# The closing stage of a streaming encoder layer: two groups of inner tiles in one sum, and a norm placed between products

## The chip, the cores and the metric

The kernel runs on one core of one Trainium2 chip. The metric is device time in microseconds (us) of one execution. TensorE (PE) multiplies matrices, VectorE (DVE), ScalarE (ACT) and GpSimd (POOL) work elementwise, and SyncE (SP) issues the transfers (DMAs).

## What is computed

One inference step of one encoder layer for 1088 tokens of width 1024 in float32. After the attention part the second feed-forward block closes the layer:

```python
h = h + 0.5 * rmsnorm(swiglu(rmsnorm(h, g_pre_ff2), w_gate2, w_up2, w_down2), g_post_ff2)
return rmsnorm(h, g_final), rows

def swiglu(x, w_gate, w_up, w_down):
    return (jax.nn.silu(x @ w_gate) * (x @ w_up)) @ w_down
```

The inner width of the block is 2816, so the hidden product has 22 tiles of 128 rows. Two norms follow the down projection: post2, which needs the whole down projection of a token, and the final one, which needs the whole of h.

## The kernel before

Activations lie transposed: features on the 128 partitions (KT = 8 tiles), tokens along the free axis. Tokens are split into G1 (576) and G2 (512). Each operand of a product is split into a high part (ACT cast, L139) and a low part (DVE subtraction, L140), so one product of tiles is three matmuls: high by high, high by low, low by high. All matmuls are issued at L154.

`ffn` is a generator that runs a feed-forward block. For each inner tile `mi` it loads four units of gate and up weights (`unit`: a DMA into one of four `wr` buffers, then cast and subtraction into one of eight `wl`/`wh` buffers), runs 48 matmuls of 512 columns, forms silu(gate) * up with three ACT and two DVE steps (L361 to L365) and splits the result into `hh`/`hl`. Inner tiles come in groups of GROUP = 4. `down` adds a group to the result y: for each of eight feature tiles `dt` it sums the group's tiles in one PSUM bank (`f`, three banks in rotation), and DVE adds the bank to y (L319). A group's `down` comes after the first tile of the next group. The last group has only the tiles 20 and 21; `down_last` adds it, and there the block of G2 is cut into two halves of 256 tokens (`step`), first half first.

The block of G2 is the last one of the kernel (`third` in `body`). When all its products are laid out, `last` lays out the norms: for each half, square and sum of y over the eight tiles (L214 to L218), a matmul with ones to sum over partitions, reciprocal root on ACT (L227, L230), the post2 scaling and the residual in place (L276 on DVE, L277 on DVE or, for odd tiles, POOL), a second norm of the result, the final scaling into an `out` buffer (L1099, two buffers of two tiles each) and its DMA (L1101). In the second half the sums over tiles are made by PE (`rms_pe`, L238 to L241).

Much earlier in the program, at the end of the attention part of G2, `L.scaled` prepares the input of that block: eight scalings (L263) into `e` buffers (three), each followed by a cast and a subtraction, on POOL for odd tiles. Another block's products run beside it as filler.

A scheduler of the language sets the order of each engine's queue from an estimate of when things are ready; the engines then run their queues strictly in that order. In the names that follow, numbers are of buffers: one number of `f` is one bank's sum.

Of the kernel before, what the change touches and what calls it, by code (L numbers as in the profile page):

```python
# [7 lines left out]
F32 = mybir.dt.float32  # L8
F32R = mybir.dt.float32r
AF = mybir.ActivationFunctionType  # L10
ALU = mybir.AluOpType
# [4 lines left out]
P = 128  # L16
D = 1024
KT = D // P
H = KT // 2
# [6 lines left out]
FT = DFF // P  # L26
# [12 lines left out]
G2 = (576, 512, 512)  # L39
# [3 lines left out]
GROUP = 4  # L43
# [22 lines left out]
class Layer:  # L66
# [225 lines left out]
    def unit(self, pool, src):  # L292
        lo = pool.tile([P, 512], F32R, name="wl")
        hi = pool.tile([P, 512], F32R, name="wh")
        raw = pool.tile([P, 512], F32, name="wr")
        self.nc.sync.dma_start(raw, src)
        self.split(hi, lo, x=raw)
        return hi, lo

    def ffn(self, pool, tmp, n, g, xhi, xlo, y, end=None, tail=None):  # L300
        nc, a = self.nc, self.a
        _, T, C = g
        wg, wu, wd = a[f"wg{n}"], a[f"wu{n}"], a[f"wd{n}"]
        pend = []

        def units(src):
            return [self.unit(pool, src[:, i:i + 512]) for i in (0, 512)]

        def product(part, ws, first, dt, c0, C):
            ps = self.bank_f()  # L310
            ks = slice(dt % H * P, dt % H * P + P)
            for i, ((wh, wl), (_, hh, hl)) in enumerate(zip(ws, part)):
                yield from self.steps(ps[:, :C], wh[:, ks], wl[:, ks], hh[:, c0:c0 + C], hl[:, c0:c0 + C],
                                      i == 0, i == len(part) - 1)
            yy = y[:, dt, c0:c0 + C]
            if first:
                nc.scalar.copy(yy, ps[:, :C])
            else:
                nc.vector.tensor_tensor(yy, ps[:, :C], yy, op=ALU.add)  # L319


        def down(part, first):
            for half in range(2):
                ws = [self.unit(pool, wd[mi][:, half * 512:half * 512 + 512]) for mi, _, _ in part]
                for dt in range(half * H, half * H + H):
                    for c0 in range(0, T, C):
                        yield from product(part, ws, first, dt, c0, C)


        def down_last(part, step, beside):  # L330
            ws = [[self.unit(pool, wd[mi][:, half * 512:half * 512 + 512]) for mi, _, _ in part] for half in range(2)]
            if step:
                order = [(dt, c0, step) for c0 in range(0, T, step) for dt in range(KT)]
            else:
                order = [(dt, c0, C) for dt in range(KT) for c0 in range(0, T, C)]
            for dt, c0, n in order:
                for _ in product(part, ws[dt // H], False, dt, c0, n):
                    yield True
                next(beside, None)

        for m in range(0, FT, GROUP):
            part = []
            for mi in range(m, min(m + GROUP, FT)):
                if mi == m + 1 and pend:
                    yield from down(pend.pop(0), m == GROUP)
                gw = units(wg[mi])
                uw = units(wu[mi])
                hh = pool.tile([P, T], F32R, name="hh")
                hl = pool.tile([P, T], F32R, name="hl")
                for c0 in range(0, T, C):  # L350
                    cs = slice(c0, c0 + C)
                    pg = self.bank_f()
                    pu = self.bank_f()
                    for ps, ws in ((pg, gw), (pu, uw)):
                        for k in range(KT):
                            wh, wl = ws[k // H]
                            ks = slice(k % H * P, k % H * P + P)
                            yield from self.steps(ps[:, :C], wh[:, ks], wl[:, ks], xhi[:, k, cs], xlo[:, k, cs],
                                                  k == 0, k == KT - 1)
                    s = tmp()[:, :C]  # L360
                    nc.scalar.activation(s, pg[:, :C], AF.Exp, scale=-1.0)  # L361
                    nc.scalar.activation(s, s, AF.Ln, bias=self.one)
                    nc.scalar.activation(s, s, AF.Exp, scale=-1.0)  # L363
                    nc.vector.tensor_tensor(s, pg[:, :C], s, op=ALU.mult)  # L364
                    nc.vector.tensor_tensor(s, pu[:, :C], s, op=ALU.mult)  # L365
                    self.split(hh[:, cs], hl[:, cs], x=s)
                part.append((mi, hh, hl))
            pend.append(part)
        while end and not self.mixed:
            yield BLOCKED  # L370
        end = end() if end else iter(())
        yield from down_last(pend.pop(0), tail, end)
        self.run(end)


# [638 lines left out]
def body(tc, a, ctx):  # L1014
    nc = tc.nc
    L = Layer(tc, ctx, a)
# [5 lines left out]
    fp = ctx.enter_context(tc.tile_pool(name="ffn", bufs=1))  # L1022
# [6 lines left out]
    F = Stream()  # L1029
# [7 lines left out]
    def pair(pool, T, name):  # L1037
        return pool.tile([P, KT, T], F32R, name=name + "h"), pool.tile([P, KT, T], F32R, name=name + "l")
# [8 lines left out]
    def ytile(T):  # L1047
        return fp.tile([P, KT, T], F32, name="y")
# [21 lines left out]
            nc.sync.dma_start(a["yT"][k * P:k * P + P, t0:t0 + T], o)  # L1070
            t = L.done(t + SLACK * (T / 960 + 0.15))

    def last(gi, y, res, pool, step):

        t0, T, C = groups[gi]
        yT = a["yT"].rearrange("(k p) t -> p k t", p=P)
        for c0 in range(0, T, step):
            cs = slice(c0, c0 + step)
            tmp = lambda: pool.tile([P, step], F32, name="t", bufs=4)

            def norm():

                r = pool.tile([P, step], F32, name="r", bufs=4)
                if c0 + step == T:
                    L.rms_pe(tmp, L.bank_f, [y[:, k, cs] for k in range(KT)], step, r)
                else:
                    for k in range(KT):
                        L.square(tmp, r, y[:, k, cs], k == 0)
                    L.rsqrt(L.bank_f, r, step, D, r)
                return r  # L1090

            r = norm()
            for k in range(KT):
                L.residual(res[:, k, cs], y[:, k, cs], "post2", k, r, None, nc.gpsimd if k % 2 else nc.vector)
            r = norm()
            for k in range(0, KT, 2):
                o = pool.tile([P, 2, step], F32, name="out", bufs=2)
                for i in range(2):
                    nc.vector.scalar_tensor_tensor(o[:, i], y[:, k + i, cs], L.gain("final", k + i), r,  # L1099
                                                   op0=ALU.mult, op1=ALU.mult)  # L1100
                nc.sync.dma_start(yT[:, k:k + 2, t0 + c0:t0 + c0 + step], o)  # L1101

    def premix(tmp, bank, y, T, hi, lo, at):
        r = L.rms(tmp, bank, [y[:, k, :] for k in range(KT)], T, D, at=at)
# [2 lines left out]
    def work(pool, T, n=4):  # L1107

        L.there = L.clock + 6.0

        class W:
            def tile(self, shape, dt, name):
                return pool.tile(shape, dt, name=name, bufs=2)
        return lambda: pool.tile([P, T], F32, name="e", bufs=n), W(), lambda: pool.tile([P, T], F32, name="acc")


    T1, T2 = G1[1], G2[1]
    x1 = pair(fp, T2, "x")
    with tc.tile_pool(name="x0", bufs=1) as xp:
        x0 = pair(xp, T1, "x")  # L1120
        y = ytile(T1)
        half = T1 // 2
        y0 = ytile(T1)
        zero = L.ffn(F, fact, 1, G1, *x0, y0)
        for c0 in (0, half):
            cs = slice(c0, c0 + half)
# [4 lines left out]
            tmp = lambda: xp.tile([P, half], F32, name="t", bufs=5)  # L1131
            r = xp.tile([P, half], F32, name="r", bufs=2)
# [10 lines left out]
        tmp = lambda: xp.tile([P, T2], F32, name="p", bufs=4)  # L1143
        get = streamed(tmp, xT[1])
        r = L.rms(tmp, L.bank_f, (get(k) for k in range(KT)), T2, D)
# [19 lines left out]
    with tc.tile_pool(name="m0", bufs=1) as mp:  # L1165
        tmp, wp, acc = work(mp, T1)
# [7 lines left out]
    tmp, wp, acc = work(mp, T1, 3)  # L1174
    o = pair(mp, T1, "o")
# [11 lines left out]
    with tc.tile_pool(name="m1", bufs=1) as mp:  # L1187
        tmp, wp, acc = work(mp, T2)
# [6 lines left out]
    h = hp.tile([P, KT, T2], F32, name="h")  # L1195
    with tc.tile_pool(name="m2", bufs=1) as mp:
        tmp, wp, acc = work(mp, T2)
        o = pair(mp, T2, "o")
        L.mix_out(wp, tmp, acc, L.bank_m, 1, G2, *o, h, rz)
    lp = ctx.enter_context(tc.tile_pool(name="last", bufs=1))  # L1200
    x3 = pair(lp, T2, "x")
    tmp = lambda: lp.tile([P, T2], F32, name="e", bufs=3)
    L.scaled(tmp, lambda k: h[:, k], "pre2", rz, *x3)
    L.run(second)

    y3 = lp.tile([P, KT, T2], F32, name="y")
    third = L.ffn(F, fact, 2, G2, *x3, y3, tail=T2 // 2)
    L.filler = third
    finish(0, y2, 2, L.bank_m)
    L.run(third)  # L1210
    last(1, y3, h, lp, T2 // 2)


OUTS = {"yT": (D, NTOK), "o_lat": (P, NTOK), "o_kr": (32, NTOK), "o_k": (512, NTOK), "o_v": (NTOK, 512)}
# [87 lines left out]
```

## Time and profile before

| | us |
|---|---|
| three timed runs: lowest, median, highest | 2359.6, 2362.08, 2370.45 |
| the profiled execution's own time | 2356.51 |
| its span, first to last instruction | 2354.7 |
| PE busy in the span | 2265.2 (96%) |
| granted TensorE clock, mean over the span | 0.990 |

The profile is one execution. Busy time of PE is of overlapping matmuls, so a stretch can be filled without a matmul starting at every moment; the distance from one start to the next is the pace. A releaser behind an arrow is what ended a wait.

### The profile page before, as it was taken

The page shows a single profiled execution, that of the slowest core. Times are in us where ns is not written, and L with a number is a line of the kernel's source. Part 1 is how long each engine was busy: PE and PEld are TensorE (multiplying, and loading weights), DVE is VectorE, ACT ScalarE, POOL GpSimd, SP SyncE. Part 2 cuts the span into 40 slices and gives each one's busy share as a digit, 9 for nine tenths or more (in the row PEclk, how much of TensorE's full clock was granted, in tenths as well). Part 3 has the DMA queues.
Part 4 walks back from the last instruction along what each step waited for, and adds up shares of the span by engine and source line. Part 5 has one row for each costly group of instructions (what it writes and reads, how often), then busy time and mean ns, then how long its engine had stood idle before and what let it go on. Part 6 is the DMA issues. An engine that isn't in the chain of part 4 may idle for free.

```text
span 2354.7 us, 37574 instructions
## 1 busy us (share of the span) xinstructions
PE 2265.2 (96%) x13841; PEld 2036.4 (86%) x13841; DVE 1433.7 (61%) x2482; ACT 1283.9 (55%) x2494; POOL 95.8 (4%) x270
## 2 busy tenths in 40 slices
PE   8999999989999999999989999999999989999996
PEld 7999999979987777788878998989898888888884
DVE  5444444764248777846874478878776568344445
ACT  6543333452357777754542588777876445433333
POOL 1000000010000000000110000000000010000001
PEclk9999999999999999999999999999999999999998
DMA  6322222444454434344445532322212334332221
GB/s 208 106 90 90 81 81 84 155 156 143 146 157 123 131 111 126 92 147 131 134 144 176 171 104 82 93 86 86 90 63 97 106 99 147 114 98 99 95 85 36
DMA packets 186615, 268.80 MB, mean 114 GB/s; under 512 B 59216, under 2 KB 68048, under 8 KB 186400
## 3 DMA queue, kind: packets, MB, share of 16 engines
q1 hardware_dynamic: 186432, 266.41, 35.1%
q8 instruction: 109, 1.79, 0.3%
q14 instruction: 74, 0.61, 0.1%
HBM read 227.61 MB, written 40.88 MB: 114 GB/s over the span
## 4 chain that ended last, share of the span: by engine, by line
PE 71%; DVE 11%; ACT 9%; DMA 4%; issue 3%; SPq 1%; POOL 1%; DVEq 0%; ACTq 0%; POOLq 0%
PE f L154 48%; PE s L154 9%; PE v L154 6%; PE t L154 6%; DVE a L613 2%; PE t L158 2%; ACT wh L139 1%; DVE wl L140 1%; ACT a L607 1%; ACT a L609 1%; DVE a L610 1%; ACT a L608 1%; DVE e L263 1%; DVE pl L680 1%; DVE y L276 1%
## 5 line engine op out<-in xcount | busy, mean ns | idle before, releaser
L154 PE MATMUL f<-xh,wh 128*128 128x288 f32 (+1 forms) x2112 | 694.3, 329 | 5.6 <-ACT xh L139 2.8
L154 PE MATMUL f<-xl,wh 128*128 128x288 f32 (+1 forms) x2112 | 695.5, 329 | 2.2 <-POOL xl L140 1.5
L154 PE MATMUL f<-xh,wl 128*128 128x288 f32 (+1 forms) x2112 | 694.7, 329 | 0.0
L139 ACT CAST wh<-wr 128x512 fp32r<-128x512 f32 x638 | 385.1, 619 | 518.1 <-PE f L154 354.7
L140 DVE TENSOR_TENSOR wl<-wr,wh 128x512 fp32r<-128x512 f32 x638 | 435.6, 698 | 256.2 <-ACT wh L139 223.7
L154 PEld LDWEIGHTS f<-xh,wh 128*128 128x128 f32 x2112 | 397.3, 188 | 36.4 <-DVE act L364 3.5
L154 PEld LDWEIGHTS f<-xl,wh 128*128 128x128 f32 x2112 | 397.1, 188 | 33.8 <-POOL xl L140 3.1
L154 PEld LDWEIGHTS f<-xh,wl 128*128 128x128 f32 x2112 | 397.2, 188 | 28.5 <-issue 1.7
L154 PE MATMUL f<-hh,wh 128*128 128x288 f32 (+2 forms) x1072 | 351.0, 328 | 8.4 <-DVE y L319 8.2
L154 PE MATMUL f<-hh,wl 128*128 128x288 f32 (+2 forms) x1072 | 351.0, 328 | 0.0
L154 PE MATMUL f<-hl,wh 128*128 128x288 f32 (+2 forms) x1072 | 350.4, 327 | 0.1
L154 PEld LDWEIGHTS f<-hh,wh 128*128 128x128 f32 x1072 | 201.9, 189 | 24.1 <-DVE y L319 9.8
L154 PEld LDWEIGHTS f<-hl,wh 128*128 128x128 f32 x1072 | 202.2, 189 | 14.5 <-issue 1.0
L154 PEld LDWEIGHTS f<-hh,wl 128*128 128x128 f32 x1072 | 202.1, 189 | 13.6 <-issue 1.0
L319 DVE TENSOR_TENSOR y<-f,y 128x288 f32<-128x288 f32 (+2 forms) x248 | 127.0, 519 | 116.9 <-PE f L154 116.6
L364 DVE TENSOR_TENSOR act<-f,act 128x288 f32<-128x288 f32 (+1 forms) x132 | 70.2, 532 | 121.1 <-ACT act L363 121.0
L680 DVE TENSOR_TENSOR pl<-t,ph 128x384 fp32r<-128x384 f32 (+1 forms) x160 | 98.7, 632 | 28.6 <-ACT ph L679 27.4
L365 DVE TENSOR_TENSOR act<-f,act 128x288 f32<-128x288 f32 (+1 forms) x132 | 70.1, 531 | 65.0 <-PE f L154 61.4
L139 ACT CAST hh<-act 128x288 fp32r<-128x288 f32 (+1 forms) x132 | 65.1, 494 | 78.7 <-DVE act L365 78.4
L154 PE MATMUL v<-pl,v 128*128 128x256 f32 x320 | 89.6, 302 | 14.8 <-DVE pl L680 13.9
L679 ACT CAST ph<-t 128x384 fp32r<-128x384 f32 (+1 forms) x160 | 84.4, 543 | 33.2 <-PE t L158 31.7
L158 PE MATMUL t<-c_ident,a 128*128 128x128 f32 x616 | 91.3, 273 | 4.9 <-ACT a L624 4.8
(316 smaller groups left out, 3476.5 us busy)
## 6 DMA issues: line engine op xcount, KB each, us to landing
wr<-in_wg SPq DMA_DIRECT2D x176, 256.0 KB, 2.7
wr<-in_wu SPq DMA_DIRECT2D x176, 256.0 KB, 3.1
wr<-in_wd SPq DMA_DIRECT2D x176, 256.0 KB, 2.7
wr<-in_win SPq DMA_DIRECT2D x44, 256.0 KB, 3.2
kl<-ks SPq DMA_DIRECT2D x64, 128.0 KB, 2.8
wr<-in_wout SPq DMA_DIRECT2D x32, 256.0 KB, 2.8
h<-y SPq DMA_DIRECT2D x16, 288.0 KB, 2.4
p<-in_xT SPq DMA_DIRECT2D x16, 256.0 KB, 3.2
```

The lines of the kernel that those rows point to most:

```text
L139: nc.scalar.copy(hi, x)
L140: eng.tensor_tensor(lo, x, f(hi), op=ALU.subtract)
L154: self.nc.tensor.matmul(out, lhsT=lhsT, rhs=rhs, start=start, stop=stop)
L158: self.nc.tensor.transpose(out, x, ident)
L263: self.nc.vector.scalar_tensor_tensor(x, src(k), self.gain(name, k), r, op0=ALU.mult, op1=ALU.mult)
L276: nc.vector.scalar_tensor_tensor(y, y, self.gain(name, k), r, op0=ALU.mult, op1=ALU.mult)
L319: nc.vector.tensor_tensor(yy, ps[:, :C], yy, op=ALU.add)
L364: nc.vector.tensor_tensor(s, pg[:, :C], s, op=ALU.mult)
L365: nc.vector.tensor_tensor(s, pu[:, :C], s, op=ALU.mult)
L613: nc.vector.tensor_tensor_scan(a[:, 0:n - 1][:, ::-1], zs[:, 1:n][:, ::-1], a[:, 0:n - 1][:, ::-1], BIG, op0=ALU.add, op1=ALU.subtract)
L679: nc.scalar.copy(ph[:, end:], tr[:, end:])
L680: nc.vector.tensor_tensor(pl[:, end:], tr[:, end:], f(ph[:, end:]), op=ALU.subtract)
```

## The change

1. In the last block (`tail` set), `down` of the group 16 to 19 is not run after tile 20. The groups 16 to 19 and 20 to 21 go to `down_last` together: each bank sums six tiles, 18 matmuls of 256 columns, for 16 banks (eight feature tiles, two halves of the tokens).
2. The twelve weight units that this takes are laid out there. Nine go into the buffer of the input pair of an earlier block (`spare`, free by then; its tiles are called `xh`/`xl`), three into the rotating `wl`/`wh`. The inner result of tile 21 gets a buffer in another pool.
3. `last` becomes a generator and is stepped once after each bank of `down_last`. While the first half's banks run, it lays out the squares of y of that half; between the banks of the second half, the root r1, the post2 step, the squares and the root r2 of the first half, and the squares of the second half. After the last bank: the root r3 of the second half (two matmuls), the final scaling of the first half, then the post2 step, norm and final scaling of the second half.
4. The `out` tiles are taken from the `e` buffers, of which there are now five; so `L.scaled` has five as well.

```diff
+        def unit(src):
+            if not room:
+                return self.unit(pool, src)
+            hi, lo = room.pop(0)
+            raw = pool.tile([P, 512], F32, name="wr")
+            nc.sync.dma_start(raw, src)
+            self.split(hi, lo, x=raw)
+            return hi, lo
...
-                if mi == m + 1 and pend:
+                if mi == m + 1 and pend and not (tail and m + GROUP >= FT):
                     yield from down(pend.pop(0), m == GROUP)
...
-                hh = pool.tile([P, T], F32R, name="hh")
-                hl = pool.tile([P, T], F32R, name="hl")
+                own = inner if inner and mi == FT - 1 else pool
+                hh = own.tile([P, T], F32R, name="hh")
+                hl = own.tile([P, T], F32R, name="hl")
...
-        yield from down_last(pend.pop(0), tail, end)
+        if spare:
+            room.extend(spare())
+        yield from down_last(sum(pend, []), tail, end)
...
+        for k in range(KT):
+            L.square(tmp, r1, y[:, k, one], k == 0)
+            yield
+        ps = None
+        for k in range(KT):
+
+            if k < KT - 1:
+                L.square(tmp, r3, y[:, k, two], k == 0)
+
+            if k == 0:
+                L.rsqrt(L.bank_f, r1, step, D, r1)
+            elif k < 5:
+                for i in range(2 * k - 2, 2 * k):
+                    moved(i, one, r1)
+                    L.square(tmp, r2, y[:, i, one], i == 0)
+            elif k == 6:
+                L.rsqrt(L.bank_f, r2, step, D, r2)
+            if k < KT - 1:
+                yield
+        sq = tmp()
+        nc.scalar.activation(sq, y[:, KT - 1, two], AF.Square)
+        ps = L.bank_f()[:, :step]
+        L.mul(ps, lhsT=L.ones, rhs=r3, start=True, stop=False)
+        L.mul(ps, lhsT=L.ones, rhs=sq, start=False, stop=True)
+        scale(ps, r3)
+        for k in range(0, KT, 2):
+            out(k, one, r2)
+        for k in range(KT):
+            moved(k, two, r3)
+        L.rms_pe(tmp, L.bank_f, [y[:, k, two] for k in range(KT)], step, r4)
+        for k in range(0, KT, 2):
+            out(k, two, r4)
...
-    tmp = lambda: lp.tile([P, T2], F32, name="e", bufs=3)
+    tmp = lambda: lp.tile([P, T2], F32, name="e", bufs=5)
```

`moved` is the post2 step (L276, L277) and `out` the final scaling with its DMA; both are as before.

PE's queue before, where the last group's banks begin (the first of the eight banks of the first half; `hh_24113` is tile 20, `hh_24357` tile 21):

```order
L154 MATMUL f_24441<-hh_24113,wh_24418 128x256
L154 MATMUL f_24441<-hl_24114,wh_24418 128x256
L154 MATMUL f_24441<-hh_24113,wl_24417 128x256
L154 MATMUL f_24449<-hh_24113,wh_24418 128x256
L154 MATMUL f_24449<-hl_24114,wh_24418 128x256
L154 MATMUL f_24449<-hh_24113,wl_24417 128x256
...
L154 MATMUL f_24441<-hh_24357,wh_24424 128x256
L154 MATMUL f_24449<-hh_24357,wh_24424 128x256
```

And after the change, from tile 20 of the first bank on (`hh_24113` is tile 20, `hh_24197` tile 21; twelve matmuls of the tiles 16 to 19 stand ahead of them in that bank):

```order
L154 MATMUL f_24313<-hh_24113,xh_24257 128x256
L154 MATMUL f_24313<-hl_24114,xh_24257 128x256
L154 MATMUL f_24313<-hh_24113,xl_24258 128x256
L154 MATMUL f_24313<-hh_24197,xh_24257 128x256
L154 MATMUL f_24338<-hh_23617,xh_24257 128x256
L154 MATMUL f_24338<-hl_23618,xh_24257 128x256
L154 MATMUL f_24338<-hh_23617,xl_24258 128x256
L154 MATMUL f_24313<-hl_24198,xh_24257 128x256
```

Before, nine matmuls of tile 20 stood ahead of the first one that needs tile 21; now fifteen do, and three more stand between the high and the low part of tile 21.

DVE's queue before, around the last bank of the second half (L319) and the first half's post2 step behind it:

```order
L319 TENSOR_TENSOR y<-f,y 128x256 x6
L276 SCALAR_TENSOR_TENSOR y<-y,c_gains,r 128x256 x2
L277 TENSOR_TENSOR y<-y,h 128x256
L276 SCALAR_TENSOR_TENSOR y<-y,c_gains,r 128x256 x2
L277 TENSOR_TENSOR y<-y,h 128x256
```

After the change, in the second half of the tokens, from the add of its second bank to that of its fifth (L331 is the bank's add, r_24334 the sum for r2, r_24335 that for r3):

```order
L331 TENSOR_TENSOR y_21650<-f_24524,y_21650 128x256
L276 SCALAR_TENSOR_TENSOR y_21650<-y_21650,c_gains_111,r_24333 128x256 x2
L218 TENSOR_TENSOR r_24335<-r_24335,t_24544 128x256
L218 TENSOR_TENSOR r_24334<-r_24334,t_24552 128x256
L277 TENSOR_TENSOR y_21650<-y_21650,h_20311 128x256
L331 TENSOR_TENSOR y_21650<-f_24555,y_21650 128x256
L276 SCALAR_TENSOR_TENSOR y_21650<-y_21650,c_gains_111,r_24333 128x256 x2
...
L331 TENSOR_TENSOR y_21650<-f_24588,y_21650 128x256
```

The post2 step of the first half now stands between the second half's bank adds, where before it stood behind all of them.

DVE's queue at the scaling of the input (L263), before the change and then after it; L319 and L331 are both the filler's bank adds:

```order
L263 SCALAR_TENSOR_TENSOR e<-h,c_gains,rx 128x512 x3
L140 TENSOR_TENSOR xl<-e,xh 128x512
L319 TENSOR_TENSOR y<-f,y 128x288
L263 SCALAR_TENSOR_TENSOR e<-h,c_gains,rx 128x512
...
L319 TENSOR_TENSOR y<-f,y 128x288 x3
L140 TENSOR_TENSOR wl<-wr,wh 128x512 x3
L319 TENSOR_TENSOR y<-f,y 128x288 x4
```

```order
L263 SCALAR_TENSOR_TENSOR e<-h,c_gains,rx 128x512 x3
L140 TENSOR_TENSOR xl<-e,xh 128x512
L263 SCALAR_TENSOR_TENSOR e<-h,c_gains,rx 128x512
...
L331 TENSOR_TENSOR y<-f,y 128x288 x3
L140 TENSOR_TENSOR wl<-wr,wh 128x512 x3
L331 TENSOR_TENSOR y<-f,y 128x288 x5
```

The one bank add that stood among the scalings now stands behind all of them.

## Rows read from the trace of the kernel before

**Rows 1.** The page: the chain that ended last, by engine.

```profile
PE 71%; DVE 11%; ACT 9%; DMA 4%; issue 3%; SPq 1%; POOL 1%; DVEq 0%; ACTq 0%; POOLq 0%
```

**Rows 2.** Stretches: us, busy PE, PEld, DVE, ACT, POOL, granted clock, DMA share, GB/s.

```profile
2272.65:2294.41 21.76, 21.76 (x98) 18.02 (x96) 10.77 (x17) 5.61 (x10) 0.00 (x0) 1.00 0.22 70
2294.41:2305.29 10.88, 10.88 (x50) 9.01 (x48) 2.58 (x4) 2.55 (x4) 0.00 (x0) 1.00 0.00 0
2305.29:2318.08 12.79, 12.53 (x97) 11.72 (x96) 9.59 (x24) 3.79 (x9) 0.00 (x0) 1.00 0.01 1
2318.08:2337.89 19.81, 7.73 (x22) 5.66 (x20) 13.18 (x28) 9.15 (x22) 3.35 (x4) 0.66 0.12 40
2337.89:2354.70 16.81, 5.71 (x16) 3.65 (x16) 9.36 (x20) 4.22 (x10) 3.37 (x4) 0.74 0.23 78
```

**Rows 3.** Timeline of PE: start, us, what; pace of matmuls, and the sums over partitions.

```profile
2309.09 0.28 PE L154 MATMUL f<-hh,wh 128*128 128x256 f32 x1
2309.21 0.28 PE L154 MATMUL f<-hl,wh 128*128 128x256 f32 x1
...
2318.08 0.59 PE L154 MATMUL f<-r,ones 128*128 128x256 f32 x2
```

**Rows 4.** The chain that ended last, in order of time: start, us, what.

```profile
2306.86 0.70 DVE hl L140
...
2318.71 0.48 ACT r L227
...
2319.22 0.42 ACT r L230
...
2329.76 7.15 PE f L154 x18
...
2346.68 0.91 DVE out L1099 x3
```

**Rows 5.** Timeline of DVE, closing stage: start, us, what, count [idle before <-releaser].

```profile
2308.15 1.09 DVE L319 TENSOR_TENSOR y<-f,y 128x256 f32<-128x256 f32 x3 [0.59 <-PE f L154]
...
2319.67 0.88 DVE L276 SCALAR_TENSOR_TENSOR y<-y,c_gains,r 128x256 f32<-128x256 f32 x2 [0.96 <-ACT r L230]
2320.47 0.42 DVE L277 TENSOR_TENSOR y<-y,h 128x256 f32<-128x256 f32 x1
2320.80 1.34 DVE L276 SCALAR_TENSOR_TENSOR y<-y,c_gains,r 128x256 f32<-128x256 f32 x2
...
2325.59 4.12 DVE L218 TENSOR_TENSOR r<-r,t 128x256 f32<-128x256 f32 x7
...
2349.87 1.67 DVE L1099 SCALAR_TENSOR_TENSOR out<-y,c_gains,r 128x256 f32<-128x256 f32 x4 [1.51 <-DMA out_yT<-out]
```

**Rows 6.** Timeline of ACT, and the page's DMA issues: a square, four weight casts, a landing.

```profile
2310.19 0.42 ACT L217 ACTIVATE t<-y 128x256 f32<-128x256 f32 x1 [0.50 <-DVE y L319]
...
2292.34 2.67 ACT L139 CAST wh<-wr 128x512 fp32r<-128x512 f32 x4 [8.22 <-PE f L154]
...
wr<-in_wd SPq DMA_DIRECT2D x176, 256.0 KB, 2.7
```

**Rows 7.** Timeline at the input's scaling, POOL, DVE and PE.

```profile
1906.54 1.29 POOL L140 TENSOR_TENSOR xl<-e,xh 128x512 fp32r<-128x512 f32 x1 [12.26 <-DMA wr<-in_wd]
...
1906.51 0.45 DVE L319 TENSOR_TENSOR y<-f,y 128x288 f32<-128x288 f32 x1
1906.88 1.50 DVE L263 SCALAR_TENSOR_TENSOR e<-h,c_gains,rx 128x512 f32<-128x512 f32 x1
...
1913.74 0.75 DVE L263 SCALAR_TENSOR_TENSOR e<-h,c_gains,rx 128x512 f32<-128x512 f32 x1 [1.16 <-POOL xl L140]
...
1915.01 1.18 DVE L319 TENSOR_TENSOR y<-f,y 128x288 f32<-128x288 f32 x3
...
1915.51 0.61 PE L154 MATMUL f<-hh,wh 128*128 128x288 f32 x1 [6.64 <-DVE y L319]
...
1915.00:1920.00 5.00, 4.49 (x20) 4.49 (x21) 3.70 (x8) 0.14 (x1) 1.28 (x1) 0.56 0.32 101
```

More of the change, by code (lines that the diff above doesn't have):

```diff
@@ L298, in unit, with ffn @@
         return hi, lo
-    def ffn(self, pool, tmp, n, g, xhi, xlo, y, end=None, tail=None):
+    def ffn(self, pool, tmp, n, g, xhi, xlo, y, end=None, tail=None, spare=None, inner=None):
         nc, a = self.nc, self.a
         _, T, C = g
+        room = []
         wg, wu, wd = a[f"wg{n}"], a[f"wu{n}"], a[f"wd{n}"]
         pend = []
+        def unit(src):
[6 more added lines that the diff above has]
+            return hi, lo
         def units(src):
@@ L330, in down_last @@
         def down_last(part, step, beside):
[L331 to L337, printed above, removed]
+            ws = [[unit(wd[mi][:, half * 512:half * 512 + 512]) for mi, _, _ in part] for half in range(2)]
+            order = [(dt, c0) for c0 in range(0, T, step) for dt in range(KT)] if step else \
+                [(dt, c0) for dt in range(KT) for c0 in range(0, T, C)]
+            for dt, c0 in order:
+                for _ in product(part, ws[dt // H], False, dt, c0, step or C):
                     yield True
@@ L1071, in finish, with last @@
             t = L.done(t + SLACK * (T / 960 + 0.15))
-    def last(gi, y, res, pool, step):
+    def last(gi, y, res, pool):
         t0, T, C = groups[gi]
+        step = T // 2
         yT = a["yT"].rearrange("(k p) t -> p k t", p=P)
[L1077 to L1101, printed above, removed]
@@ new lines, in last, with scale, moved, out @@
+        tmp = lambda: pool.tile([P, step], F32, name="t", bufs=4)
+        row = lambda: pool.tile([P, step], F32, name="r", bufs=4)
+        def scale(ps, r):
+            nc.scalar.activation(r, ps, AF.Ln, bias=L.eps, scale=1.0 / D)
+            nc.scalar.activation(r, r, AF.Exp, scale=-0.5)
+        def moved(k, cs, r):
+            L.residual(res[:, k, cs], y[:, k, cs], "post2", k, r, None, nc.gpsimd if k % 2 else nc.vector)
+        def out(k, cs, r):
+            o = pool.tile([P, 2, step], F32, name="e", bufs=5)
+            for i in range(2):
+                nc.vector.scalar_tensor_tensor(o[:, i], y[:, k + i, cs], L.gain("final", k + i), r,
+                                               op0=ALU.mult, op1=ALU.mult)
+            nc.sync.dma_start(yT[:, k:k + 2, t0 + cs.start:t0 + cs.stop], o)
@@ new lines, in last @@
+        one, two = slice(0, step), slice(step, T)
+        r1, r2, r3, r4 = row(), row(), row(), row()
+        for k in range(KT):
[15 more added lines that the diff above has]
+                yield
@@ L1103, in premix @@
+        yield
     def premix(tmp, bank, y, T, hi, lo, at):
@@ L1206, in body, with spare @@
     y3 = lp.tile([P, KT, T2], F32, name="y")
-    third = L.ffn(F, fact, 2, G2, *x3, y3, tail=T2 // 2)
+    def spare():
+        both = [z.rearrange("p k t -> p (k t)") for z in pair(fp, T1, "x")]
+        return [[z[:, i:i + 512] for z in both] for i in range(0, KT * T1, 512)]
+    third = L.ffn(F, fact, 2, G2, *x3, y3, end=lambda: last(1, y3, h, lp), tail=T2 // 2, spare=spare, inner=lp)
     L.filler = third
@@ L1210, in body @@
     L.run(third)
-    last(1, y3, h, lp, T2 // 2)
 OUTS = {"yT": (D, NTOK), "o_lat": (P, NTOK), "o_kr": (32, NTOK), "o_k": (512, NTOK), "o_v": (NTOK, 512)}
```

## The prediction

> **What bounds the kernel now.** The chain by engine comes first [rows 1]: PE makes 71% of it. The change touches the end of the program, so the stretches there come next [rows 2]. Up to 2318.08 PE is full at clock 1.00; from there to the end, 36.6 us, it is not the bound. Two stretches make up that end: 19.81 us until the post2 step of the second half of the tokens begins, and 16.81 us from there. The first one is the whole norm work of the first half and the second half's r3, and in it DVE is busy for 13.18 us. The second half's last products are done at 2318.08, yet its post2 step starts only at 2337.89, because the first half's work stands ahead of it in DVE's queue. The chain in order of time says the same [rows 4]: ACT's root at 2318.71, DVE until the ones-matmul at 2329.76, then PE, then DVE again. While the products of the first half run, DVE and ACT have room: in the 12.79 us of the last group's banks ACT is busy for 3.79. That is the time the change wants to use.
>
> **1. PE's products.** Before: 96 matmuls of 512 columns for the tiles 16 to 19, 21.76 us, and 96 of 256 columns for 20 and 21 in 12.79 us [rows 2]. The pace of 256 columns is 0.12 us [rows 3], so those 96 need 11.5 us; the other 1.3 us is PE waiting for tile 21's split, whose low part ends at 2307.56 [rows 4], 2.27 us after that tile's own products end. After: 288 of 256 columns, 34.56 us, and two ones-matmuls among them (r1, r2) at 0.59 each with their latency [rows 3], together 35.7. Before it was 34.55: plus 1.2 us. The wait for tile 21 should go: the order puts fifteen matmuls ahead of its high part (1.8 us) and nineteen ahead of its low part (2.28 us against 2.27 needed). If that fails, it costs 0.2. The Trainium skill (page TensorE: Matmul & The Clock Gate, section Back-to-back issue gap) gives columns divided by 2.4 GHz plus 2.5 ns for a warm matmul, 109 ns for 256 columns; the row shows 120 and decides; by the page this term would be 2.0 us less.
>
> **2. The weights.** Twelve units (DMA, cast, subtraction) in one go, where before eight were spread over `down` and four followed. Their number and bytes are the same. Nine go into a buffer nobody uses any more, so their casts wait only for a transfer (2.7 us to landing [rows 6]) and not for PE, as the casts of before do (8.22 us [rows 6]). In ACT's order they stand beside tiles 19 and 20, so at least 10.88 us, one tile's time [rows 2], ahead of the first use. Cost 0, covered by tile 21's products; without that cover see the rivals.
>
> **3. The first half's norm beside the second half's products.** Eight banks of 18 matmuls, 2.16 us each. r1's ones-matmul comes after the first of them, r2's after the seventh: 0.59 + 6 x 2.16 = 13.55 us from one to the other. If r2's sum isn't ready by then, PE stands. From r1's ones-matmul: 0.59, root 0.48 + 0.42 [rows 4], 1.5 with handovers. Then DVE: before, the eight scalings and four adds of that step, three of four pairs slowed by a POOL add running beside them (1.34 for a pair against 0.88 [rows 5]), took from 2319.67 to 2325.6, 6.0 us. Between them now stand seven sums for r2, four for r3 and four bank adds, fifteen at about 0.335 (three adds fill 1.09 [rows 5]; the distance of starts): 5.0. The last squares and their chained sums add about 1.0: 4.12 us for seven chained sums [rows 5] makes 0.53 each, and a square takes 0.42 [rows 6]. Sum 13.5 against 13.55. So the wait is between 0 and, with every handover adverse, 1.5 us; I take 0.4, near the lower end, since both sums come out alike. Before that, the bank ring has slack: each of the three banks is needed again two banks (4.3 us) after its end, and DVE's lag never reaches 3.
>
> The four POOL adds of that step run in a stretch where POOL was idle; what they cost is inside the 1.34 rows.
>
> **4. From the last product to the second half's post2 step.** Before 19.81 us [rows 2]. After: three final scalings of the first half stand ahead of the last bank add in DVE's queue. r2's root comes 0.59 + 0.48 + 0.42 and a square between (0.3) after the seventh bank, 1.85 us with handovers; three scalings at 0.4 make 3.05, where the last bank's matmuls end 2.75 after the same point. So the bank add starts 0.3 late; then add 0.42, square 0.42, ones-matmul 0.59, roots 0.90, six handovers of about 0.04: 2.9 us in all. The five final scalings left (2.0 us) fit behind it. With the chance that one of them is late I take 3.3; bounds 2.6 and 5. Gain 19.81 - 3.3 = 16.5 us.
>
> **5. The end.** From 2337.89 to the first final scaling at 2346.68 [rows 4] nothing changes. The eight scalings then took until 2351.5, 4.9 us, with a wait of 1.51 for an `out` buffer on its way to memory [rows 5]. With five `e` buffers they run through: 7 x 0.4 + 0.48 = 3.3. Gain 1.6; if the four transfers of 256 KB, now closer together, queue behind each other, up to 0.7 of it is lost. DMA's 3.1 us at the very end stays.
>
> **6. The five `e` buffers at the input's scaling.** This is a place the change moves without naming it. There PE stood 6.64 us waiting for a filler bank add that is queued behind the scalings [rows 7]. With more buffers the last scaling no longer waits 1.16 us for POOL, so the group of adds may come about 1.0 sooner, near 1914.0. But the single add that stood among the scalings at 1906.51 moves behind them too. It freed a bank, with which PE ran twelve matmuls until 1908.9 (where its wait of 6.64 begins). They now come after the wait: 1.6 us at their pace, nearly 3 at the half clock that follows the wait (0.56 over 1915 to 1920 [rows 7]). Net between 0.5 us won (the clock recovers sooner as PE resumes sooner) and 2 lost; I take 1.0 lost.
>
> **Sum.** +1.2 + 0.4 - 16.5 - 1.6 + 1.0 = -15.5 us. The profiled execution (2356.51; 1.8 around the span of 2354.7) would take 2341.0. It lies 5.6 us under the median of the three runs, which I take as base: 2362.08 - 15.5 = **2346.6 us**, 0.66% faster. About 0.5%, 11.8 us, is what a measurement can tell from no change.
>
> **Rivals.**
> *DVE becomes the bound of the second half.* If POOL slows every DVE operation beside it as it does the scaling of 0.75 us that took 1.50 [rows 7], and not one per POOL add, the 8 + 4 + 15 operations of step 3 grow: four POOL adds of 0.84 us, each holding two operations for about 0.45 more, plus the chain behind them, 4 to 5 us; PE stands at r2's ones-matmul. Gain 11: 2351, within 0.5%. For: 13.5 against 13.55 leaves nothing. Against: only one operation per pair is longer in the rows of before [rows 5].
>
> *The weights come late.* If the casts could not run ahead, six units stand between tile 21 and the first bank: 2.7 for the transfer and 6 x 0.67 of cast (2.67 for four [rows 6]) make 6.7 us of idle PE. Gain 8.8: 2353. Against: the order, and free buffers.
>
> *The clock falls in the long sums, and the kernel gets slower.* The banks of `down_last` wait for DVE in a ring of three, and DVE now does norms between. If the short waits make the clock fall to 1.2 GHz, a matmul of 256 columns takes about 0.21 instead of 0.12 (at clock 0.56 twelve products took nearly twice their time, above). All 288: plus 26 us, 2362.1 + 10.7 = 2373. It is slower than before once more than some 170 of the 288 run so. Against: in the 12.79 us of before, same columns, same ring and a wait of 1.3, the clock was 1.00 [rows 2]; it fell only in long waits. The Trainium skill (the same page, section A second HAM failure mode: psum-queue depth-cycling) says that cycling through banks with short idle pauses can make the clock swing. By that rule this rival would be likely; the trace disagrees.
>
> *The change doesn't do what it says*: the norm still runs after the products, because of a wait that I have not seen. Then 1.2 lost and 1.6 + 1.3 won: 2361, no difference.
>
> **How the numbers follow.** Forecast (gain 13 to 18) 79%; DVE bound 8%; weights late 5%; norm not beside 3%; clock 3%; 2% for what I don't see, half of it slower. Half of the DVE case lies above 11.8 us. Faster 0.82, same 0.14, slower 0.04. The bounds of the terms make the gain 11 to 18; with a base between 2359.6 and 2364 the time is 2341 to 2353; I widen it by 1 on both sides: 2340 to 2354, which leaves out the norm and clock cases and a part of the weights.
>
> **What would show it.** In the changed kernel's trace: matmuls of 256 columns without a break for about 35.5 us; L276 of the first half between bank adds; PE's wait at the second ones-matmul (0 to 1.5, step 3); 3 to 4 us from the last product to the second half's first L276 (step 4); no wait of the final scalings for a DMA (step 5); PE's wait near 1907 to 1915, its length and the clock behind it (step 6). Wrong it would be if PE shows waits of several us among the 288 matmuls, or a clock below 1.00 there, or the end after the last product is longer than 22 us.

## The result, and the profile after

The changed kernel takes 2345.86 us (median of 5 runs, 2343.77 to 2350.41) against 2362.08 before: ratio 0.9935, 95% interval 0.9922 to 0.9949. In a second series the same kernel took 2344.72 us against 2358.91: ratio 0.9945 (0.9931 to 0.9960). The profiled execution took 2345.05 us, its span is 2343.3 against 2354.7.

The two profiled executions can't be compared by their ends alone. At 1894 us, in code that is the same in both, the one of after is already some 5 us later than that of before (before's profiled time lies 5.6 us under its median, after's 0.8), so the changed stretches are compared from a point of their own. For the end of the program this is the start of `down_last`. From there to the end the kernel of after needs 54.41 us (2288.86 to 2343.27). Before, the same products and all that stands behind them took 21.76 us for tiles 16 to 19 and 49.4 from 2305.29 to 2354.70 [rows 2], 71.2 in all. **The gain there is 16.8 us**, and that length hardly varies between executions (54.39 in a second one of the same kernel, 54.41 in one of experiment 6, which has the same end).

Stretches of the kernel after, columns as in [rows 2]: the first half's products, the second half's, from the last product to the second half's post2 step, and the rest.

```profile
2288.86:2306.60 17.74, 17.74 (x148) 17.64 (x147) 7.03 (x16) 3.54 (x8) 0.00 (x0) 1.00 0.00 1
2306.60:2324.60 18.00, 18.00 (x148) 17.89 (x147) 14.16 (x35) 7.34 (x20) 4.42 (x4) 1.00 0.00 1
2324.60:2328.02 3.42, 1.15 (x4) 0.35 (x3) 3.20 (x10) 1.31 (x3) 0.00 (x0) 1.00 0.47 158
2328.02:2343.30 15.28, 5.86 (x16) 3.52 (x16) 9.26 (x20) 4.22 (x10) 3.36 (x4) 0.70 0.31 102
```

PE is busy without a break for both halves of the sum, at clock 1.00, and DVE is busy for 14.16 us inside the second one, with norm work and bank adds (0.42 us each). The stretch of 19.81 us of before [rows 2], counted like it from the ones-matmul behind the last product (2324.42), has shrunk to 3.60.

PE's timeline of after at the two sums of the first half and of r3 (start, us, what). Neither ones-matmul shows a wait:

```profile
2308.44 0.59 PE L154 MATMUL f<-r,ones 128*128 128x256 f32 x2
...
2321.70 0.28 PE L154 MATMUL f<-hh,wl 128*128 128x256 f32 x1
2321.82 0.62 PE L154 MATMUL f<-r,ones 128*128 128x256 f32 x2
...
2324.42 0.63 PE L154 MATMUL f<-r,ones 128*128 128x256 f32 x2
```

DVE's timeline of after (the idle time ahead of an operation and what ended it in brackets): the first half's post2 step between bank adds, r2's last two sums, the final scalings ahead of the last bank add, the second half's first scaling, and the end.

```profile
2310.19 0.88 DVE L276 SCALAR_TENSOR_TENSOR y<-y,c_gains,r 128x256 f32<-128x256 f32 x2 [1.12 <-ACT r L230]
2310.98 0.42 DVE L277 TENSOR_TENSOR y<-y,h 128x256 f32<-128x256 f32 x1
2311.32 0.42 DVE L331 TENSOR_TENSOR y<-f,y 128x256 f32<-128x256 f32 x1
2311.65 1.03 DVE L276 SCALAR_TENSOR_TENSOR y<-y,c_gains,r 128x256 f32<-128x256 f32 x2
...
2320.74 0.95 DVE L218 TENSOR_TENSOR r<-r,t 128x256 f32<-128x256 f32 x2 [0.21 <-ACT t L217]
...
2324.22 1.27 DVE L1105 SCALAR_TENSOR_TENSOR e<-y,c_gains,r 128x256 f32<-128x256 f32 x3
2325.40 0.42 DVE L331 TENSOR_TENSOR y<-f,y 128x256 f32<-128x256 f32 x1
...
2328.02 0.88 DVE L276 SCALAR_TENSOR_TENSOR y<-y,c_gains,r 128x256 f32<-128x256 f32 x2 [0.22 <-ACT r L1097]
...
2336.80 3.26 DVE L1105 SCALAR_TENSOR_TENSOR e<-y,c_gains,r 128x256 f32<-128x256 f32 x8 [2.78 <-ACT r L241]
```

r2's last sum ends at 2321.69, and PE comes to r2's ones-matmul at 2321.82: 0.13 us to spare. The eight final scalings at the end run through in 3.26 us, with no wait for a transfer as in [rows 5].

ACT's timeline of after, around r2's root:

```profile
2322.48 0.48 ACT L227 ACTIVATE r<-f,eps 128x256 f32<-128x256 f32 x1
2323.42 0.42 ACT L217 ACTIVATE t<-y 128x256 f32<-128x256 f32 x1 [0.46 <-DVE y L331]
2323.75 0.40 ACT L230 ACTIVATE r<-r 128x256 f32<-128x256 f32 x1
```

A square of the second half stands between the root's two operations, and it waits 0.46 us for DVE's bank add. That time is on the way to the final scalings at 2324.22 twice over: the root ends at 2324.15, and the sum of that square, which waits for it too, stands right ahead of the scalings in DVE's queue.

```profile
2323.87 0.43 DVE L218 TENSOR_TENSOR r<-r,t 128x256 f32<-128x256 f32 x1 [0.54 <-ACT t L217]
```

The place that the change moves without naming it, the input's scaling: DVE and PE of after, to be read against [rows 7].

```profile
1909.22 2.07 DVE L263 SCALAR_TENSOR_TENSOR e<-h,c_gains,rx 128x512 f32<-128x512 f32 x3
...
1913.07 4.09 DVE L263 SCALAR_TENSOR_TENSOR e<-h,c_gains,rx 128x512 f32<-128x512 f32 x3
...
1917.69 1.75 DVE L263 SCALAR_TENSOR_TENSOR e<-h,c_gains,rx 128x512 f32<-128x512 f32 x1
...
1919.96 1.18 DVE L331 TENSOR_TENSOR y<-f,y 128x288 f32<-128x288 f32 x3
```

```profile
1920.46 0.61 PE L154 MATMUL f<-hh,wh 128*128 128x288 f32 x1 [8.08 <-DVE y L331]
```

Five `e` buffers let three scalings run in one go beside POOL's subtractions (4.09 us for three), and all bank adds come behind the last of them. PE waits 8.08 us instead of 6.64.

### The profile page after: what moved, and what is told of

It is laid out like the page before. It is cut to its first block, busy times and chain, and to the rows that moved or that the text cites. A ratio compares the mean times of both kernels' runs of the same rounds, so it can differ in the third digit from the quotient of the medians.

```text
span 2343.3 us, 37720 instructions
## 1 busy us (share of the span) xinstructions
PE 2260.2 (96%) x13925; PEld 2036.9 (87%) x13925; DVE 1432.1 (61%) x2480; ACT 1282.0 (55%) x2494; POOL 97.1 (4%) x270
## 5 line engine op out<-in xcount | busy, mean ns | idle before, releaser
L139 ACT CAST wh<-wr 128x512 fp32r<-128x512 f32 x629 | 379.9, 619 | 496.3 <-PE f L154 329.6
L154 PE MATMUL f<-hh,wh 128*128 128x288 f32 (+2 forms) x1032 | 337.0, 327 | 9.4 <-DVE y L331 9.3
L154 PE MATMUL f<-hh,wl 128*128 128x288 f32 (+2 forms) x1032 | 337.5, 327 | 0.0
L154 PE MATMUL f<-hl,wh 128*128 128x288 f32 (+2 forms) x1032 | 336.3, 326 | 0.0
L154 PEld LDWEIGHTS f<-hh,wh 128*128 128x128 f32 x1032 | 194.9, 189 | 23.5 <-DVE y L331 10.9
L154 PEld LDWEIGHTS f<-hl,wh 128*128 128x128 f32 x1032 | 195.1, 189 | 13.1 <-issue 1.0
L154 PEld LDWEIGHTS f<-hh,wl 128*128 128x128 f32 x1032 | 195.2, 189 | 12.6 <-issue 1.0
L331 DVE TENSOR_TENSOR y<-f,y 128x288 f32<-128x288 f32 (+2 forms) x240 | 121.6, 513 | 115.9 <-PE f L154 115.4
```

Source lines behind the costliest of these rows:

```text
L139: nc.scalar.copy(hi, x)
L154: self.nc.tensor.matmul(out, lhsT=lhsT, rhs=rhs, start=start, stop=stop)
```

## The experiments

All are edits of the changed kernel. Their stretch from the first product of `down_last` to the end is given beside the total, since it hardly varies between executions of the same end; before and after have 71.2 and 54.4.

**1. The common sum alone.** `down_last` takes the six tiles, but the norm of the first half stands behind all products.

```diff
-    third = L.ffn(F, fact, 2, G2, *x3, y3, end=lambda: last(1, y3, h, lp), tail=T2 // 2, spare=spare, inner=lp)
+    third = L.ffn(F, fact, 2, G2, *x3, y3, tail=T2 // 2, spare=spare, inner=lp)
     L.filler = third
     finish(0, y2, 2, L.bank_m)
     L.run(third)
+    last(1, y3, h, lp, T2 // 2)
```

(`last` is here the one of before, with five `e` buffers for its output.)

> The six tiles are summed together and first half first, as in the changed kernel, but the norm of the first half stands behind all products again, as before. Theory (the gain is the norm work that lies beside products): the 288 products take 34.6 us as before, the stretch from the last product to the second half's post2 step is back at 19 to 20 us, the end keeps its 1.5 us (five out buffers): 1 to 2 us under the kernel before, about 2360.5, no difference that counts. Rival (the common sum itself saves waits and bank adds): 8 us or more under before, 2354 or less.

Measured: 2358.52 us against 2359.55 before in that series, ratio 0.9995 (0.9985 to 1.0004). The chain that ended last, in order of time:

```profile
2254.80 64.85 PE f L154 x421
...
2319.67 0.48 ACT r L227
...
2338.65 0.88 DVE y L276 x2
```

From r1's root to the second half's post2 step it takes 18.98 us, before 19.18 (2318.71 [rows 4] to 2337.89 [rows 2]). The closing stretch is 69.6 us: 1.6 gained, at the end of the output. The common sum by itself brings next to nothing beyond what the five buffers bring; the rival falls.

**2. The norm alone.** Tiles 16 to 19 are summed in `down` again, and only tiles 20 and 21 lie beside the norm.

```diff
-                if mi == m + 1 and pend and not (tail and m + GROUP >= FT):
+                if mi == m + 1 and pend:
...
-    third = L.ffn(F, fact, 2, G2, *x3, y3, end=lambda: last(1, y3, h, lp), tail=T2 // 2, spare=spare, inner=lp)
+    third = L.ffn(F, fact, 2, G2, *x3, y3, end=lambda: last(1, y3, h, lp), tail=T2 // 2)
```

> Tiles 16 to 19 are summed by themselves again, and only tiles 20 and 21 (0.72 us a bank) stand beside the norm of the first half. Theory: r1's to r2's ones-matmul needs 13.5 us of DVE and ACT, and 0.59 + 6 x 0.72 = 4.9 us of products lie between, so PE waits some 8.6 us before the last bank; tile 21's wait of 1.3 is back too. From the end of tile 21: 1.3 + 5.8 + 0.7 + 13.5 + 1.3 + 3.3 = 25.9 us against 32.6 before, and 1.5 at the end: 8 us under before, about 2354, half the gain. Rival (the norm hides as well beside 96 products, the longer sum is not needed): 15 us or more, 2347 or less.

Measured: 2355.78 us against 2359.55, ratio 0.9978 (0.9969 to 0.9988), 2.8 to 7.3 us. PE's timeline:

```profile
2315.42 0.70 PE L154 MATMUL f<-r,ones 128*128 128x256 f32 x2 [0.85 <-DVE r L218]
...
2319.68 0.39 PE L154 MATMUL f<-hh,wh 128*128 128x256 f32 x1 [0.70 <-DVE y L331]
...
2321.81 0.39 PE L154 MATMUL f<-hh,wh 128*128 128x256 f32 x1 [1.15 <-DVE y L331]
...
2329.00 1.22 PE L154 MATMUL f<-r,ones 128*128 128x256 f32 x2 [6.21 <-DVE r L218]
```

From r1's ones-matmul to r2's it takes 13.58 us, where 13.5 was expected, and PE waits in three places (0.70, 1.15, 6.21: 8.06 of the expected 8.6). With tiles 16 to 19 added as before (21.76) the closing stretch is 65.5 us: 5.7 gained, a third and not the half. The 2.6 us that the expectation lacked from tile 21 to the second half's post2 step (28.5 for 25.9) lie almost all at its two ends: r1's ones-matmul already waits 0.85, and the stretch from r2's ones-matmul to the post2 step takes 6.15 instead of 4.6, in which PE, behind the wait of 6.21, runs at half clock.

```profile
2315.42:2329.00 13.58, 5.52 (x39) 4.86 (x39) 12.14 (x30) 6.08 (x17) 3.03 (x4) 0.90 0.00 0
2329.00:2335.15 6.15, 4.58 (x12) 2.95 (x12) 4.29 (x11) 2.32 (x6) 0.00 (x0) 0.50 0.28 95
```

These stretches of the same execution (columns as above) show DVE busy for 12.14 of the 13.58 us, and a clock of 0.50 behind the wait. So the norm needs the long sum as a cover, and the long sum needs the norm: 1.6 and 5.7 apart, 16.8 together, each with the 1.5 us in it that the five buffers give at the end.

**3. r2 one bank earlier.** It measures how much room r2's sum has.

```diff
-            elif k == 6:
+            elif k == 5:
                 L.rsqrt(L.bank_f, r2, step, D, r2)
```

> r2's ones-matmuls stand one bank (2.16 us) earlier in PE's order, all else as in the changed kernel. Theory (r2's sum is ready 0.13 us before PE comes to it, so the fifteen operations of DVE just fit): PE now waits 2.0 us there; the last bank's add no longer stands behind three scalings, which gives back 0.3 to 0.7: 1.3 to 2 us slower than the changed kernel, about 2347.5. Rival (the sum is ready much earlier and DVE only takes its time): a wait under 0.7, and the time is that of the changed kernel or 0.5 us less.

Measured: 2346.95 us, ratio 0.9939 (0.9927 to 0.9952); the closing stretch is 55.9 us, 1.5 more than after. PE:

```profile
2323.12 0.70 PE L154 MATMUL f<-r,ones 128*128 128x256 f32 x2 [1.92 <-DVE r L218]
...
2327.97 0.59 PE L154 MATMUL f<-r,ones 128*128 128x256 f32 x2
```

The wait is 1.92 us; one bank less the 0.13 of room is 2.03. From the last product (r3's ones-matmul, 2327.97) to the second half's post2 step (2330.88) it is 2.9 us instead of 3.6, since r2's scalings no longer stand in front of the last bank add. The fit of step 3 was a close one; the totals of two kernels that differ by 1.5 us could not have shown it.

**4. No POOL in the last norm.** All adds of the last post2 steps on DVE.

```diff
-            L.residual(res[:, k, cs], y[:, k, cs], "post2", k, r, None, nc.gpsimd if k % 2 else nc.vector)
+            L.residual(res[:, k, cs], y[:, k, cs], "post2", k, r, None, nc.vector)
```

> The adds of the last post2 steps all run on DVE, none on POOL, in both halves; all else as in the changed kernel. Theory (a POOL add slows one DVE operation of a pair from 0.48 to 0.94, which is what the adds cost DVE anyway): scalings 0.48 throughout, four adds of 0.335 more on DVE in each half: PE's wait at r2 stays 0, the time from the second half's first scaling to its first final scaling changes by less than 0.7, the total lies within 1 us of the changed kernel, 2345 to 2347. Rival (POOL's share sets the end: without it DVE is the bound): r2 late by 1.3 and the end longer by 1.3, 2348 to 2349.

Measured: 2343.31 us, ratio 0.9926 (0.9913 to 0.9938). In the timeline of DVE the pairs of scalings now take 0.88 us and each pair of adds 0.75; with POOL a pair of scalings took up to 1.34 us and the one add left on DVE 0.41.

```profile
2322.27 0.88 DVE L276 SCALAR_TENSOR_TENSOR y<-y,c_gains,r 128x256 f32<-128x256 f32 x2 [0.22 <-ACT r L1097]
2323.06 0.75 DVE L277 TENSOR_TENSOR y<-y,h 128x256 f32<-128x256 f32 x2
```

The closing stretch is 54.55 us, 0.14 more than after: what POOL takes off DVE it costs DVE in longer scalings. The median lies 2.55 us under after's first one and below the 2345 to 2347 expected, but the stretch that the edit touches doesn't show it, and the intervals overlap; I count it as no difference. PE's timeline shows a wait of 0.19 us at r2, so the room there is used up either way:

```profile
2316.57 0.70 PE L154 MATMUL f<-r,ones 128*128 128x256 f32 x2 [0.19 <-DVE r L218]
```

**5. Three `e` buffers again.** It undoes step 6 and leaves the rest.

```diff
-            o = pool.tile([P, 2, step], F32, name="e", bufs=5)
+            o = pool.tile([P, 2, step], F32, name="out", bufs=3)
...
-    tmp = lambda: lp.tile([P, T2], F32, name="e", bufs=5)
+    tmp = lambda: lp.tile([P, T2], F32, name="e", bufs=3)
```

> Three e buffers at the input's scaling again, and the out tiles of the last norm in three buffers of their own; all else as in the changed kernel. At the scaling one bank add comes back among the scalings. Theory (step 6 costs about 1 us): PE's wait there falls from 8.1 to 6.6 and the stretch up to the first product behind the scalings gets about 1.3 shorter; the end is longer by 0.7, since the fourth pair of the final scalings waits for a transfer: in sum 0 to 1 us faster than the changed kernel, 2345 to 2346. Rival (step 6 costs nothing): 0.7 to 1 slower, 2346.5. The total can hardly tell them apart, the two places in the trace can.

Beside it ran the changed kernel once more:

> The changed kernel itself, beside the other runs of this series: 2344 to 2348 us, ratio 0.9935 as before.

Measured: 2344.21 us against 2344.72 for the changed kernel (and 2358.91 before), ratios 0.9937 (0.9926 to 0.9949) and 0.9945 (0.9931 to 0.9960): no difference. PE's wait at the scaling is 6.64 us again, and the next product there comes 1.4 us sooner, measured against the changed kernel on the same chip (3.8 us ahead of it in front of the scaling, 5.2 behind). But at 2007 us the lead is down to 3.4: it was given back. Where it went is told below. At the end the last pair of scalings waits for an output buffer:

```profile
2333.03 2.46 DVE L1105 SCALAR_TENSOR_TENSOR out<-y,c_gains,r 128x256 f32<-128x256 f32 x6 [2.77 <-ACT r L241]
2336.22 0.88 DVE L1105 SCALAR_TENSOR_TENSOR out<-y,c_gains,r 128x256 f32<-128x256 f32 x2 [0.73 <-DMA out_yT<-out]
```

That is 0.73 us, against 1.51 with two buffers [rows 5] and none with five; the closing stretch is 55.4 us, 1.0 more than after.

*Where the lead goes.* Some 70 us behind the scaling PE waits 2.2 to 2.6 us for a sum over `tmp` (`finish` of the first group). PE's timeline there, first of before, then of after:

```profile
1987.05 0.75 PE L154 MATMUL t<-tmp,ones 128*128 128x288 f32 x2 [2.21 <-DVE tmp L218]
...
1989.41 0.63 PE L154 MATMUL f<-xh,wl 128*128 128x512 f32 x1
1989.84 0.63 PE L154 MATMUL f<-xh,wh 128*128 128x512 f32 x1
```

```profile
1994.00 0.75 PE L154 MATMUL t<-tmp,ones 128*128 128x288 f32 x2 [2.52 <-DVE tmp L218]
...
1995.54 0.39 PE L154 MATMUL f<-xh,wl 128*128 128x512 f32 x1
1995.77 0.40 PE L154 MATMUL f<-xh,wh 128*128 128x512 f32 x1
```

The starts lie 0.43 us apart in the one and 0.23 in the other: half and full clock. The five us from that point have a mean granted clock of 0.66 before, 0.66 in experiment 5, 1.00 after:

```profile
1987.00:1992.00 5.00, 4.95 (x14) 3.88 (x15) 3.95 (x6) 2.28 (x5) 0.00 (x0) 0.66 0.35 114
```

```profile
1988.40:1993.40 5.00, 5.00 (x15) 3.83 (x16) 3.72 (x6) 2.28 (x5) 0.00 (x0) 0.66 0.35 111
```

```profile
1994.00:1999.00 5.00, 5.00 (x22) 4.10 (x23) 4.05 (x7) 2.81 (x6) 0.00 (x0) 1.00 0.40 125
```

Fourteen or fifteen matmuls run in five us where 22 do at full clock: there the lead of experiment 5 falls from 5.0 to 3.4, by 1.6 us. So the longer wait of after at the scaling costs 1.4 us on the spot, and in these executions the shorter one is followed by a loss of 1.6 at half clock. That the one brings on the other is not shown.

**6. The scalings spread out.** If PE's 8 us at the scaling are on the path, bank adds between the scalings should give them back.

```diff
-    L.scaled(tmp, lambda k: h[:, k], "pre2", rz, *x3)
+    for k in range(KT):
+        L.scaled(tmp, lambda k: h[:, k], "pre2", rz, *x3, ks=[k], pace=False)
+        for _ in range(24):
+            next(second, None)
```

> The eight scalings of the input no longer stand in one block: behind each of them come 24 steps of the products of the inner group, so that in DVE's order their bank adds stand between the scalings; all else as in the changed kernel. Theory (PE's 8.1 us at the scalings are on the path): the wait falls below 1 us and the half clock behind it goes, 6 to 9 us faster than the changed kernel, 2337 to 2340. Rival (DVE's queue behind it is the bound: the sums of the final norm of the first group, for which PE waits 2.5 us at 1994, come no earlier): the wait moves to that place, less than 2 us gained, 2344 to 2346.

Measured: 2336.29 us, ratio 0.9904 (0.9891 to 0.9917); the changed kernel in the same series had 2344.72. DVE's timeline has bank adds between the scalings, and PE's longest wait there is 1.20 us:

```profile
1910.37 0.81 DVE L331 TENSOR_TENSOR y<-f,y 128x288 f32<-128x288 f32 x2
1911.10 1.04 DVE L263 SCALAR_TENSOR_TENSOR e<-h,c_gains,rx 128x512 f32<-128x512 f32 x1
1912.06 0.44 DVE L331 TENSOR_TENSOR y<-f,y 128x288 f32<-128x288 f32 x1
```

```profile
1910.87 0.40 PE L154 MATMUL f<-hh,wh 128*128 128x288 f32 x1 [1.20 <-DVE y L331]
```

Against the changed kernel on the same chip the lead grows from 2.7 us in front of the scaling to 10.5 behind it, 7.8 us, and falls to 8.9 at the sum over `tmp`, where the clock is 0.66 again. So by the traces this edit is worth 6.2 us; the other 2.7 us between these two executions lie in front of the scaling, in code that is the same (the medians are 8.4 apart). The closing stretch is the same 54.4. The wait of 1.20 is not quite the "below 1 us" of the theory, and the median lies 0.7 under its range; but the wait at the sum over `tmp` is still 2.2 us, so the rival's move of the wait did not occur. The theory holds: those 8 us were on the path.

**7. Both.** Scalings spread, and no POOL in the last norm.

> Both edits together: the scalings spread among bank adds, and no add of the last post2 steps on POOL. If they are independent, the time is that of the spread scalings less 0 to 2 us: 2336 to 2340 by the first theory, 2342 to 2345 by its rival.

Measured: 2333.53 us (2332.94 to 2336.07), ratio 0.9894 (0.9882 to 0.9907), 25 us under the kernel before of that series and 2.8 under experiment 6, which is more than the 0 to 2 expected. It is the lowest median of the study. But the closing stretch is 54.2 us: of the 1.8 us between the two profiled executions only 0.2 lie where the second edit acts, and 1.6 ahead of the sum of six tiles, in code that is the same.

## Why the prediction was right, and where it was not

It said 2346.6 us, by a sum of -15.5. The medians give -16.2 in the first series and -14.2 in the second, the trace -16.8 for the closing stretch and about 0 for step 6. So the sum is right to about 1.3 us; that the first median lies within 0.8 us of the forecast is partly luck, since the medians of before alone range from 2358.9 to 2362.1. The parts:

| step | predicted | measured |
|---|---|---|
| 1. products, first to last | 35.7 + 0.4, against 34.55 | 35.56 |
| 3. PE's wait at r2 | 0.4 (0 to 1.5) | 0 |
| 4. last product to second post2 | 3.3 (2.6 to 5), against 19.81 | 3.60 |
| 5. the end | -1.6 | -1.55 |
| 6. the input's scaling | +1.0 (-0.5 to 2) | +1.4, given back 70 us later |

**Step 1** was right, pace and all: 288 matmuls at 0.12 make 34.56, and the other 1.0 us of the 35.56 is mostly the two ones-matmuls; the trace shows no wait for tile 21. The 109 ns that the prediction quotes from the Trainium skill (page TensorE: Matmul & The Clock Gate, section Back-to-back issue gap) are, by that section, the gap of a matmul by itself; in this stream it is 120 ns, so the 2.0 us worked out from them say nothing of this sum. **Step 2**: the last casts of the weights end 10 us ahead of the first use at 2288.86:

```profile
2278.20 0.62 ACT L139 CAST wh<-wr 128x512 fp32r<-128x512 f32 x1 [0.46 <-PE f L154]
```

**Step 3** was 13.5 against 13.55 on paper and 13.25 against 13.38 in the trace. Its terms were less exact than its sum: r1's root took 1.75 us (2308.44 to 2310.19) for 1.5, the DVE work behind it 11.5 for 12.0. That PE found the sum ready, by 0.13 us, is thus luck; that the two come out alike is not. This is the mechanism of the whole change, and three runs bear it out: with the cover cut to 4.9 us PE waited 8.06 (experiment 2), with the cover a bank shorter 1.92 (3), and with the cover but no norm in it the 19 us behind the products stayed (1).

**Step 4** was off by 0.3, and the term that was mis-sized is the way from r2's ones-matmul to the first final scaling: "1.85 us with handovers" was 2.40 (2321.82 to 2324.22). I had put a square of 0.3 between the root's two operations, but not that this square waits 0.46 us for a bank add, nor that its sum stands ahead of the scalings in DVE's queue. In experiment 4 the square finds its bank add done: there the way takes 1.90 us (2316.57 to 2318.47), and from r3's ones-matmul to the post2 step it is 3.0 us instead of 3.6. An operation laid between two others in a queue brings its own wait with it.

**Step 5** was right: 2336.80 to 2343.27 is 6.47 us, before 8.02 (2346.68 [rows 4] to 2354.70). The transfers don't queue up: from the end of the last scaling to the end of the program it is 3.2 us in both kernels. And three buffers instead of five cost 1.0 in experiment 5, 0.73 of it in that wait.

**Step 6** was the weakest. The adds were to begin 1.0 us sooner; it was 0.35, because three scalings in one go beside POOL take 4.09 us. The single add that moved behind the scalings cost about what was said. That the 1.4 us came back later, where the clock stayed full, was not foreseen. It makes this term about 0 instead of +1.0, which is most of what the sum missed.

**The rivals.** *DVE as the bound of the second half* did not occur, but by 0.13 us only. The price of the four POOL adds is in sum that of [rows 5] (three pairs, 0.46 us each): two pairs of scalings take 1.02 and 1.03 instead of 0.88, two pairs of sums 1.29 instead of 0.76, 1.35 us in all. It falls in part on the sums, which the prediction had at their own pace. Experiment 4 shows that it cancels against the adds that POOL takes over. *Late weights*: not seen. *The clock in the long sums*: 1.00 in both halves, as over the shorter sum of before [rows 2], though the bank adds now stand between norm work in DVE's queue. The Trainium skill (page TensorE: Matmul & The Clock Gate, section A second HAM failure mode: psum-queue depth-cycling) tells of a kernel whose clock swings because PE pauses briefly between groups of matmuls while it cycles through banks. Over these 35.6 us PE cycled through three banks but made no pause, so this trace doesn't test it; in the 12.79 us of before [rows 2], with 1.3 us of waits, the clock was 1.00 all the same. *The change doesn't do what it says*: experiment 1 is that case, and it measured 2358.52 against 2359.55, no difference, as that rival's "2361, no difference" says. (The chances listed for the cases add up to 0.83 for faster, not 0.82; nothing hangs on it.)

## What to carry to other kernels

Work that follows the products can be laid beside them only as far as the products are long enough: write down the chain that has to fit (here 13.3 us) and the products that cover it (13.4), and lengthen the cover if it is short; the halves alone gave 1.6 and 5.7 of the 16.8 us. Look beyond the stretch that is changed: a pool's buffer count moved bank adds at a place 370 us ahead of the changed stretch, and the wait found there was worth another 6 us. Compare two traces stretch by stretch from a common point, since ends of single executions differ by several us for other reasons.

## What the runs showed of the hardware that was not expected

**The same wait is followed by half clock or by full clock.** At the sum over `tmp` PE waits 2.2 to 2.6 us in every kernel. In before and in experiments 5, 6 and 7 the five us behind it have a mean clock of 0.66; in after (two executions) and in experiments 1 to 4 it is 1.00. The first four are those whose wait at the scaling, 70 us earlier, is 6.64 or 1.20 us, the other six those with 8.08. Four of four and none of six is hardly chance, but PE was busy in between, and no run here shows what links the two. It is left open.

**POOL's share is paid mostly by DVE, one operation at a time.** A pair of scalings of 256 columns takes 0.88 us alone and 1.34 where a POOL add runs beside it [rows 5]; one of 512 columns takes 0.75 us [rows 7] and beside POOL up to 1.75 (input's scaling of after). A sum of 256 columns (two inputs from SBUF) takes 0.42 us alone and 0.96 beside a POOL add. Bank adds, of whose two inputs one comes from PSUM, take 0.41 to 0.42 (256 columns) beside POOL as without. Once, in every kernel with this order, it is POOL that pays: an add of 0.85 takes 1.86 us while DVE's sums and adds beside it keep their 0.42. Both, from after:

```profile
2312.61 1.29 DVE L218 TENSOR_TENSOR r<-r,t 128x256 f32<-128x256 f32 x2
2315.28 0.76 DVE L218 TENSOR_TENSOR r<-r,t 128x256 f32<-128x256 f32 x2
2315.44 1.86 POOL L277 TENSOR_TENSOR y<-y,h 128x256 f32<-128x256 f32 x1 [1.82 <-DVE y L276]
```

No run shows what decides who pays. The Trainium skill (GPSIMD Engine Reference, section 1. Specifications) says that POOL shares its SBUF interfaces with DVE and contends with operations of two SBUF inputs; the runs agree, and experiment 4 adds the price: laying every second add on POOL gained DVE nothing.
